# A two-block layer kernel: the one-hot rows that enter the weight-building products are first copied to one contiguous run per token

## The chip, the core and the metric

One core of one Trainium2 chip. The time is device microseconds of one execution; the median of three runs of the kernel before is 2320.74 us. Beside it stands one profiled execution. Engines are named as the profile names them: PE (TensorE matmul), PEld (TensorE weight load, overlapping PE), DVE (VectorE), ACT (ScalarE), POOL (GpSimd), SP (SyncE, which issues most loads).

## The reference

Two transformer blocks, one after the other, on one sequence of 512 tokens of width 1024. The change lies in the last part of the second block, a product-key mixture of single-neuron experts (PEER):

```
q = (xb @ w_query).reshape(TOKEN_BLOCK, P_HEADS, 2, P_HALF)
s = einsum('thpk,hpnk->thpn', q, sub_keys)
sv, si = top_k(s, P_TOPK)
... eidx: the 16 best of the 256 pairs of each of 8 heads; g: softmax of their scores
u = u_tab[eidx]
act = gelu(einsum('td,thkd->thk', xb, u))
return einsum('thk,thkd->td', g * act, v_tab[eidx])
```

There are 16384 experts; an expert number is a pair of two numbers below 128, and each token picks 8 x 16 of them.

## The kernel before, in words

All matrix products run on PE with operands split into a high and a low part (32-bit, three products for one), except the ones of this change, which take 16-bit operands.

The experts are done in two ways. For the first 128 tokens, rows of `u_tab` and `v_tab` are gathered (line 1484) and multiplied on DVE (lines 1492 and 1510). For the other 384 tokens (three tiles b = 1, 2, 3 of 128), all 16384 experts are computed densely. `dense_S` (line 1570) makes one S tile: it loads 128 rows of `u_tab`, ACT casts the high part `uh` (1575), POOL makes the low part `ul` (1576), PE runs 24 products of 384 columns (lines 331, 332, 334) and ACT applies gelu (1580). Of the 128 S tiles, 59 are made ahead of the second product (`more_S`), and wait on chip or in DRAM (`Sd`). The second product (line 1826) multiplies each S tile by the weight that each token gives each expert and by `v_tab`.

That weight of every expert per token, a matrix of 128 x 128 for each of 384 tokens, is what the changed code builds. For 16 tokens at a time, four at a time within them:

- `make(b, n)` (line 1601): DVE writes `oh` (line 1612), for both halves of the expert number the one-hot row over 128 candidates, 4 tokens side by side in the innermost dimension, and `ow` (line 1615), the first half's one-hot row times the score in two 16-bit parts. Four instructions of each per call; four buffers each (`OB`).
- `build(b, n)` (line 1618): for each four tokens, PE runs 8 products (line 1626) of 128 x 128 into one bank `gps`: the stationary operand is a token's second one-hot row, the moving one a part of `ow`. Both are read with a step of 4 elements (8 bytes), since 4 tokens lie side by side. ACT evacuates the bank into `gst` (line 1628), and ACT's queue stores 16 tokens to DRAM (`Gd`, line 1629).

24 builds make 96 banks and 768 products. The loop at line 1702 makes the rows for the next build, then builds the present one, then asks for 3, 2 or 1.5 S tiles (b = 1, 2, 3), and for b = 1 and 2 also runs one head of the next tile's top-16 search on DVE (`topk_head`). At the end of each tile's search, `route_end` transposes the numbers on PE (1647, 1648), and ACT and DVE make `tT` (1649 to 1651), from which the next `make` reads. In b = 3 at n = 4 the gathered rows still waiting are used up on DVE (line 1492).

The order in which each engine runs its instructions is fixed before the run by the tile framework's planner, from its own estimates of cost; it need not be that of the code (in the trace `oh`, `oh`, `ow`, `ow` alternate in pairs, where the code has `oh`, `ow`). `pin` keeps some in the code's order. Each engine runs its queue in order and waits on semaphores.

```
for k in range(2):                                            # 1624
    for t in range(4):
        PE.matmul(ps[:, t * 128:(t + 1) * 128], o[:, 1, :, t], w[:, k, :, t], start=k + t == 0,
                  stop=k + t == 4, skip_group_check=True)     # 1626
S.mul(st[:, :, t4 * 4:t4 * 4 + 4], ps.rearrange("p (t i) -> p i t", i=128), 1.0 / GS)   # 1628
```

Of the kernel before, what the change touches and what calls it, by code (L numbers as in the profile page):

```python
# [11 lines left out]
F16 = mybir.dt.float16  # L12
# [8 lines left out]
D = 1024  # L21
KC = 8
SEQ = 512
META = 16
T = 512
# [3 lines left out]
LA = 6  # L29
# [8 lines left out]
GLAG = 3  # L38
# [61 lines left out]
def layout(a):  # L100
    """the inputs in the order in which the kernel reads them: feature-major activations, weights in blocks of 128
    or 256 columns, one column per 128 entries of a vector"""
# [44 lines left out]
def tile_blocks(  # L147
# [26 lines left out]
    # ---------------------------------------------------------------- constants  # L174
# [72 lines left out]
    def small_constants():  # L247
        nc.scalar.dma_start(out=cf, in_=a["cf"])
        with tc.tile_pool(name="init", bufs=1) as ip:
# [4 lines left out]
            # sqrt(w^2 + eps) of the first block's last norm  # L254
# [28 lines left out]
    # ---------------------------------------------------------------- matrix products  # L283
# [12 lines left out]
    def weights(w, m, n, eng=None, step=None):  # L296
        """a block [128, m, n] of weights and its split, step of the m at a time"""
# [14 lines left out]
    def ahead(w, hi, lo, eng=None, step=None):  # L312
        """a block of 128 columns split ahead of its turn, in other room than that of the weights"""
# [13 lines left out]
    def chain(ps, ab, first=True, last=True):  # L327
        """sum of a^T b over the pairs of split operands (a, b); a's low parts are needed last"""
# [7 lines left out]
    def gemm_fm(ws, X, N, evac, kouter=None, after=None, mid=None, eng=lambda s: None):  # L336
        """feature-major: evac(s, psum[128, N]) per block s of 128 columns; the first two blocks step by step together
        where kouter, the kind of their banks (their operand X is just coming in); after(s, raw weights);
        mid(k) after step k of these; eng(s): which engine makes the low parts of the weights"""
# [23 lines left out]
    def meta_fm(raw, um):  # L363
        """feature-major projection of the 16 meta tokens: psum[128, 16]"""
        ps = tr_tile("meta")
        for k in range(KC):
            PE.matmul(ps[:, 0:META], raw[:, k, :], um[:, k, :], start=(k == 0), stop=(k == KC - 1))
        return ps[:, 0:META]

    def gemm_tm(w, X, evac, after=None, n=256):  # L370
        """token-major: evac(b, psum[128 tokens, n]) for the n columns of w [128, KC, n]; one b per step"""
# [16 lines left out]
    def newton(ps, eps, n):  # L388
        """ps [128, n]: sums of D squares; -2 D / sqrt(ps / D + eps), its logarithm's estimate refined once"""
# [10 lines left out]
    def newton_small(ss, eps, n, tmp):  # L400
        """ss [128, m] SBUF: sums of n squares -> 1 / sqrt(ss / n + eps) in ss"""
# [8 lines left out]
    class SquareSum:  # L410
        """sums over the features of (x * wcol)^2: all chunks but the last are added up on the way"""
# [34 lines left out]
    def scaled_X(xr, wcol):  # L446
        """split of xr * wcol"""
# [5 lines left out]
    class Early:  # L453
        """two blocks of weights times X that still lacks the factor and the shift of its norm: flush(s) adds what the
        shift brings and evacuates"""
        def __init__(self, ws, X, cols, shift, evac, room, factor):
            """shift [128, KC]; room(s): two tiles of half a block's size; factor() makes the norm's factor"""
# [26 lines left out]
    def norm_X(X, xr, rs, wcol, bcol, keep=None):  # L484
        """split of xr * rs * wcol + bcol (wcol carries the factor of rs)"""
# [15 lines left out]
    def modulation(ip):  # L501
        """one step per call of next: rows of ada_w"""
# [25 lines left out]
        for n in range(6 * D // AW):  # L528
# [11 lines left out]
            # the sum over the partitions: 32 at a time by a transpose, the four of them by a product  # L540
# [17 lines left out]
    # ---------------------------------------------------------------- block 1  # L558
# [13 lines left out]
    def sigmoid(dst, src):  # L572
        """exp(-ln(1 + exp(-src))), src at least -43"""
# [4 lines left out]
    def gla(X, um, Y, sp, rs, rsT, hooks):  # L578
        """returns the parts in the order in which they may run; rs, rsT: factors of the columns and rows of products
        with X"""  # L580
# [35 lines left out]
        def decay():  # L616
            # decay: running sums of log sigmoid, restarted every 128 tokens
# [15 lines left out]
        def proj_v(h):  # L633
            """the values; with the first half of their columns, the 16 of the decay's first product"""
# [27 lines left out]
        def state():  # L662
            # state after the meta tokens
# [1202 lines left out]
```

## Time and profile before

| | us |
|---|---|
| three runs | 2320.26, 2320.74, 2330.18 |
| their median | 2320.74 |
| span of the profiled execution, first to last instruction | 2316.9 |
| median less span | 3.8 |
| busy on PE, DVE, POOL, ACT in the profiled execution | 2196.2, 1781.6, 1031.0, 903.7 |
| busy of line 1626 in it (768 products) | 98.0 |

The profile gives no other time of its own execution than the span. It is read by stretches: the builds lie between 1106 and 1420 us of the span; before it stand the other layers, behind it the second product up to the end. A matmul's end in the trace is modelled, so the pace of PE is read from starts.

### The profile page before, as it was taken

How to read it: one execution, taken by the hardware profiler on the slowest of the kernel's cores; microseconds unless marked ns; L12 is line 12 of the kernel's file. 1: busy time of each engine (PE TensorE's matmuls, PEld its weight loads, DVE VectorE, ACT ScalarE, POOL GpSimd, SP SyncE). 2: the span in 40 equal slices, each digit the busy share in tenths (PEclk: the TensorE clock that was granted, in tenths of full speed). 3: DMA queues.
4: the chain of work that ended last, by engine and by line, in shares of the span. 5: the costliest groups of instructions: out<-in, count | busy, mean ns of one | idle time of the engine just before them, and what ended most of it. 6: DMA issues, size and time to landing. Idle time of an engine off the chain costs nothing.

```text
span 2316.9 us, 30890 instructions
## 1 busy us (share of the span) xinstructions
PE 2196.2 (95%) x11067; PEld 1865.7 (81%) x11067; DVE 1781.6 (77%) x3276; ACT 903.7 (39%) x1529; POOL 1031.0 (44%) x609
## 2 busy tenths in 40 slices
PE   9999999999989999997979999999999999999996
PEld 7777777877768777776969998776789999999994
DVE  5876657654485787899999965565679998989987
ACT  3345542233334664533334443333333333333333
POOL 1310221121150003512334434777788787778776
PEclk9999999999999999998989999999999999999998
DMA  5111357553222212631545667888889999999983
GB/s 178 59 39 46 118 161 244 179 168 106 81 92 78 64 61 85 227 98 62 186 135 189 212 222 238 285 264 281 273 316 327 338 336 322 340 339 330 340 305 136
DMA packets 181268, 455.09 MB, mean 196 GB/s; under 512 B 16597, under 2 KB 82006, under 8 KB 178042
## 3 DMA queue, kind: packets, MB, share of 16 engines
q1 hardware_dynamic: 82080, 252.58, 32.7%
q0 software_dynamic: 36864, 134.23, 16.2%
q10 hardware_dynamic: 62170, 66.30, 8.3%
q8 instruction: 87, 1.43, 0.3%
q14 instruction: 67, 0.55, 0.1%
HBM read 412.63 MB, written 39.79 MB: 195 GB/s over the span
## 4 chain that ended last, share of the span: by engine, by line
PE 42%; DVE 25%; issue 16%; POOL 9%; DMA 5%; ACT 2%; ACTq 0%; POOLq 0%; DVEq 0%; SPq 0%
PE do L1826 6%; POOL gt L1484 5%; PE mm L331 4%; PE mm L332 3%; PE mm L334 3%; POOL vl L1807 3%; PE S L331 3%; PE S L332 3%; PE S L334 3%; DVE oh L1612 3%; PE ff L331 2%; PE ff L334 2%; PE ff L332 2%; DVE ow L1615 2%; DVE vacc L1510 1%
## 5 line engine op out<-in xcount | busy, mean ns | idle before, releaser
L331 PE MATMUL S<-xhi,uh 128*128 128x384 f32 x1024 | 355.8, 347 | 5.9 <-ACT sg L1580 4.7
L332 PE MATMUL S<-xlo,uh 128*128 128x384 f32 x1024 | 352.4, 344 | 0.0
L1576 POOL TENSOR_TENSOR ul<-ur,uh 128x1024 fp32r<-128x1024 f32 x59 | 157.7, 2677 | 289.8 <-ACT uh L1575 208.6
L289 DVE TENSOR_TENSOR wlo<-raw,whi 128x1024 fp32r<-128x1024 f32 (+4 forms) x150 | 175.6, 1175 | 129.9 <-ACT whi L288 100.4
L1826 PE MATMUL do<-vh,wl 128*128 128x512 f32 x768 | 245.7, 399 | 15.2 <-DVE wl L1814 15.1
L1826 PE MATMUL do<-vl,wh 128*128 128x512 f32 x768 | 245.9, 400 | 10.9 <-POOL vl L1807 10.7
L1826 PE MATMUL do<-vh,wh 128*128 128x512 f32 x768 | 245.9, 400 | 1.1 <-ACT vh L1806 0.9
L1510 DVE SCALAR_TENSOR_TENSOR vacc<-gt,act,vacc 128x1024 f32<-128x1024 f32 x127 | 211.0, 1661 | 41.9 <-DMA gt<-in_v_dram,eidx 40.2
L288 ACT CAST whi<-raw 128x1024 fp32r<-128x1024 f32 (+4 forms) x152 | 146.1, 969 | 231.9 <-PE ff L332 107.2
L1492 DVE SCALAR_TENSOR_TENSOR gt<-gt,h2t 128x1024 f32<-128x1024 f32 x118 | 176.4, 1503 | 65.3 <-DMA gt<-in_u_dram,eidx 65.1
L331 PE MATMUL mm<-xhi,whi 128*128 128x512 f32 x544 | 219.8, 404 | 0.7 <-DVE xc L1127 0.7
L1575 ACT CAST uh<-ur 128x1024 fp32r<-128x1024 f32 x128 | 134.4, 1050 | 215.5 <-DMA ur<-in_ut_dram 115.0
L332 PE MATMUL mm<-xlo,whi 128*128 128x512 f32 x544 | 217.2, 399 | 0.0
L1807 POOL TENSOR_TENSOR vl<-vr,vh 128x1024 fp32r<-128x1024 f32 x64 | 174.8, 2732 | 80.7 <-ACT vh L1806 72.7
L331 PEld LDWEIGHTS S<-xhi,uh 128*128 128x128 f32 x1024 | 199.0, 194 | 9.5 <-ACT sg L1580 5.0
L332 PEld LDWEIGHTS S<-xlo,uh 128*128 128x128 f32 x1024 | 198.8, 194 | 3.2
L334 PE MATMUL S<-xhi,ul 128*128 128x384 f32 x1024 | 201.1, 339 | 0.0
L1807 POOL TENSOR_TENSOR vl<-vx,vh 128x1024 fp32r<-128x1024 f32 x64 | 169.3, 2645 | 61.5 <-ACT vh L1806 60.7
L1813 ACT CAST wh<-sg 128x384 fp32r<-128x384 f32 x128 | 65.5, 513 | 316.9 <-PE do L1826 210.1
L1826 PEld LDWEIGHTS do<-vh,wl 128*128 128x128 f32 x768 | 145.1, 190 | 53.6 <-DVE wl L1814 20.7
L1826 PEld LDWEIGHTS do<-vl,wh 128*128 128x128 f32 x768 | 145.7, 191 | 50.8 <-POOL vl L1807 17.0
L1484 POOL DMA_INDIRECT gt<-in_v_dram,eidx x128 | 166.7, 1303 | 32.5 <-issue 25.4
(481 smaller groups left out, 4819.8 us busy)
## 6 DMA issues: line engine op xcount, KB each, us to landing
ur<-in_ut_dram SPq DMA_DIRECT2D x128, 512.0 KB, 5.5
raw<-in_w_ff_dram SPq DMA_DIRECT2D x64, 512.0 KB, 3.6
vr<-in_v_dram SPq DMA_DIRECT2D x64, 512.0 KB, 4.6
vx<-in_v_dram SPq DMA_DIRECT2D x64, 512.0 KB, 7.6
aw<-in_ada_w_dram SPq DMA_DIRECT2D x64, 384.0 KB, 3.8
Gd<-gst ACTq DMA_DIRECT2D x24, 1024.0 KB, 4.3
gti<-Gd ACTq DMA_DIRECT2D x90, 256.0 KB, 5.0
raw<-in_w_in_dram SPq DMA_DIRECT2D x32, 512.0 KB, 4.4
```

The costliest lines, as they stand in the source:

```text
L288: S.copy(hi, src)
L289: (eng or V).tensor_tensor(out=lo, in0=src, in1=hi.bitcast(F32), op=OP.subtract)
L331: PE.matmul(ps, ah, bh, start=first and i == 0, stop=False, skip_group_check=True)
L332: PE.matmul(ps, ah, bl, start=False, stop=False, skip_group_check=True)
L334: PE.matmul(ps, al, bh, start=False, stop=last and i == n - 1, skip_group_check=True)
L1484: pin(G.indirect_dma_start(out=gt, out_offset=None, in_=tab, in_offset=bass.IndirectOffsetOnAxis(ap=eidx[:, s:s + 1], axis=0)))
L1492: ins = V.scalar_tensor_tensor(gt, gt, 1.0, h2t, op0=OP.mult, op1=OP.mult, accum_out=act[:, s:s + 1])
L1510: V.scalar_tensor_tensor(vacc, gt, act[:, s:s + 1], vacc, op0=OP.mult, op1=OP.add)
L1575: S.copy(uh, ur)
L1576: eng.tensor_tensor(out=ul, in0=ur, in1=uh.bitcast(F32), op=OP.subtract)
L1807: G.tensor_tensor(out=vl, in0=vr, in1=vh.bitcast(F32), op=OP.subtract)
L1826: PE.matmul(po[2 * tb + h], w[:, ts], v[:, h * 512:(h + 1) * 512], start=first and n == 0, stop=last and n == 127, skip_group_check=True)
```

## The change

In `make`, a tile `oc` [128, 4, 128] of 16-bit entries with four buffers is added, and an ACT copy that reads the second one-hot rows (step of 4 elements) and writes each token's 128 entries in one run. `build` takes the stationary operand from `oc`. The loops over the two parts and the four tokens are exchanged: a token's two products, with the same stationary operand, follow each other. The moving operand is read as before. The first and last product of a bank are the same ones. The diff also blanks comments, which changes no instruction; lines behind 1616 move down by three.

```diff
                 w = gp.tile([128, 2, 128, 4], F16, name="ow", bufs=OB)
                 V.tensor_tensor(out=w, in0=o[:, 0:1].to_broadcast([128, 2, 128, 4]), in1=cols(2, 2), op=OP.mult)
-                made.append((o, w))
+
+                oc = gp.tile([128, 4, 128], F16, name="oc", bufs=OB)
+                S.copy(oc, o[:, 1].rearrange("p i t -> p t i"))
+                made.append((oc, w))
...
-                for k in range(2):
-                    for t in range(4):
-                        PE.matmul(ps[:, t * 128:(t + 1) * 128], o[:, 1, :, t], w[:, k, :, t], start=k + t == 0,
+                for t in range(4):
+                    for k in range(2):
+                        PE.matmul(ps[:, t * 128:(t + 1) * 128], o[:, t, :], w[:, k, :, t], start=k + t == 0,
                                   stop=k + t == 4, skip_group_check=True)
```

## Rows read from the trace of the kernel before

**Rows 1.** The page, part 1: busy time, share of the span, instructions.

```profile
PE 2196.2 (95%) x11067; PEld 1865.7 (81%) x11067; DVE 1781.6 (77%) x3276; ACT 903.7 (39%) x1529; POOL 1031.0 (44%) x609
```

**Rows 2.** Windows by stretch: stretch, its us, busy per engine, TensorE clock, DMA.

```profile
1099.00:1203.00 104.00, 99.66 (x615) 95.01 (x616) 103.96 (x288) 37.97 (x60) 40.75 (x15) 0.94 0.51 178
1203.00:1216.50 13.50, 0.33 (x3) 0.04 (x1) 13.50 (x71) 3.02 (x4) 2.35 (x1) 0.54 0.06 12
1217.00:1304.80 87.80, 87.80 (x565) 86.47 (x564) 87.73 (x310) 39.24 (x59) 42.01 (x14) 0.98 0.56 198
...
1324.00:1378.00 54.00, 53.46 (x349) 52.41 (x350) 32.23 (x44) 22.25 (x34) 16.79 (x7) 0.97 0.70 242
1378.00:1405.00 27.00, 22.29 (x155) 21.41 (x153) 25.87 (x26) 11.14 (x19) 15.37 (x6) 0.94 0.68 234
1405.00:1432.00 27.00, 27.00 (x160) 26.78 (x158) 13.40 (x21) 10.08 (x16) 9.61 (x4) 0.93 0.57 199
1432.00:2317.00 885.00, 844.13 (x4000) 730.50 (x3998) 713.86 (x726) 305.57 (x425) 673.58 (x377) 0.98 0.86 301
```

**Rows 3.** Waits, 1100 to 1432: who waited for whom, us, times, longest.

```profile
POOL ul L1576 <- ACT uh L1575: 175.2, 33, 15.3
...
PE tr L1647 <- DVE ef L1407: 13.2, 1, 13.2
PE gps L1626 <- DVE ow L1615: 12.7, 10, 2.5
```

**Rows 4.** Waits, 1324 to 1432, the same columns.

```profile
DVE oh L1612 <- PE gps L1626: 22.0, 7, 7.3
...
PE gps L1626 <- DVE ow L1615: 6.4, 3, 2.5
```

**Rows 5.** Chain that ended last, 1324 to 1432: start, us, what.

```profile
by line: PE gps L1626 23.2%; PE S L331 18.4%; PE S L332 18.1%; PE S L334 16.7%; DVE oh L1612 9.7%; DVE gv L1492 7.3%; DVE ow L1615 4.5%; DVE gt L1492 2.1%; issue 0.1%
...
1336.49 3.81 PE gps L1626 x32
...
1348.64 3.80 PE gps L1626 x32
...
1387.11 7.84 DVE gv L1492 x6
```

**Rows 6.** Line 1626: ns min/median/max, first and last start, forms.

```profile
L1626 PEld LDWEIGHTS <-oh x768: 112/117/152, 1105.8 to 1418.9; 128*128 128x128 f16 x192
```

**Rows 7.** Line 1663, the same columns: a load of 32-bit columns.

```profile
L1663 PEld LDWEIGHTS ks<-skT,q x128: 186/192/339, 946.7 to 1057.3; 128*128 128x128 f32 x128
```

**Rows 8.** Timeline from 1399.0, PEld: the first two loads of a build.

```profile
1398.99 0.15 PEld L1626 LDWEIGHTS <-oh 128*128 128x128 f16 x2 [2.51 <-DVE ow L1615]
```

**Rows 9.** Timeline of PE from 1217.2, after an idle stretch: start, us, what.

```profile
1217.22 1.48 PE L1626 MATMUL gps<-ow,oh 128*128 128x128 f16 x11
...
1219.24 0.52 PE L331 MATMUL S<-xhi,uh 128*128 128x384 f32 x1
```

**Rows 10.** Windows around it: stretch, us, busy, clock (after POOL).

```profile
1217.20:1218.50 1.30, 1.30 (x14) 1.28 (x11) 1.30 (x10) 1.02 (x4) 0.00 (x0) 0.50 0.31 122
...
1336.30:1340.00 3.70, 3.70 (x33) 3.62 (x32) 2.52 (x2) 2.29 (x4) 2.39 (x1) 1.00 0.50 169
```

**Rows 11.** Timeline of PE from 1344.3: two products of an S tile.

```profile
1344.31 0.34 PE L331 MATMUL S<-xhi,uh 128*128 128x384 f32 x1
1344.48 0.34 PE L332 MATMUL S<-xlo,uh 128*128 128x384 f32 x1
```

**Rows 12.** Costliest groups of ACT: count | busy, mean ns | idle, releasers.

```profile
L1628 ACT ACTIVATE gst<-gps 128x512 f32<-128x512 f32 x96 | 55.1, 600 | 36.2 <-PE gps L1626 32.0 <-DMA Gd<-gst 3.1 <-ACT sx L1580 0.9
...
L288 ACT CAST yhi<-Y 128x512 fp32r<-128x512 f32 x16 | 9.0, 619 | 3.1 <-DVE Y L819 2.8 <-PE tr L1249 0.3
```

**Rows 13.** Line 1612, columns as for line 1626: the one-hot rows on DVE.

```profile
L1612 DVE TENSOR_TENSOR oh<-io,tT x96: 666/683/2902, 1101.1 to 1410.2; 128x1024 f16<-128x1024 f16 x96
```

**Rows 14.** Timeline of ACT from 1344.5: a cast for a later S tile.

```profile
1344.90 1.04 ACT L1575 CAST uh<-ur 128x1024 fp32r<-128x1024 f32 x1
```

## The prediction, made before the result was known

> **What bounds the kernel now.** I read the page first: PE is busy for 2196.2 us of 2316.9, DVE for 1781.6, ACT for 903.7 [rows 1]. That is an average; what the change is worth is read from the stretches in which the builds run. The windows by stretch [rows 2] show three kinds of time. From 1099 to 1304.8 us DVE is busy in every microsecond (103.96 of 104.00, 13.50 of 13.50, 87.73 of 87.80): it makes the one-hot rows and runs the top-16 search of the next tile. PE works beside it, nearly full, and then stands still for 13 us from 1203 to 1216.5. The waits [rows 3] say why: its longest wait is 13.2 us, in the transposes of `route_end`, for the search on DVE. All its other waits there (12.7 us, 10 times) are for `ow`, again DVE. DVE's waits for PE, 22.0 us in 7 times, all lie behind 1324 [rows 4]. So up to about 1324 DVE sets the pace, and a faster PE would only wait longer.
>
> From 1324 on it is the other way round, as the search is over: PE is busy 53.46 of 54.00 us while DVE idles, then a stretch of 27 us in which DVE uses up gathered rows, then 27.00 of 27.00 on PE, and 844 of 885 us in the second product [rows 2]. The chain of waits from 1324 to 1432 has line 1626 as its largest part, 23.2% of 108 us, which is 25 us [rows 5]. One build there takes 3.81 us for 32 products, 119 ns each; so 25 us are about 208 of the 768 products. The other 560 lie where DVE sets the end. That number, **208 products**, is what any change of PE's pace in the builds is multiplied by.
>
> **Part 1: the stationary operand becomes contiguous.** What sets the 119 ns? A record of a 16-bit load lasts 112 to 117 ns [rows 6], almost the pace, so the load looks guilty. Three rows speak against it. First, a load of the same 128 columns in 32 bits, contiguous, lasts 186 ns at the least [rows 7]: the strided 16-bit load is already 74 ns shorter. Second, where a build begins after a wait, two loads are issued at once and both are over 0.15 us after the first began [rows 8]; one alone takes 0.112, so the second needs the load path for not more than 38 ns. A path that can take a load every 38 ns doesn't set a pace of 119. Third, the pace doesn't follow PE's clock: after the idle stretch, at a granted clock of 0.50 (the lower level, 1.2 GHz), 11 products take from 1217.22 to the next line's start in the same 0.11 to 0.12 us each as at 1.00 (2.4 GHz) [rows 5, 9, 10], while the S tile's products behind them last 0.52 us instead of 0.34 [rows 9, 11]. What is left is something fixed in time: the reading of the moving operand, which has the same step of 8 bytes and keeps it, the issue of a load and a product by turns, or a product that waits for the whole latency of its load. Only the last could gain from contiguous weights.
>
> The bounds: at best the pace becomes that of the columns themselves. Two products of 384 columns start 0.17 us apart [rows 11], 0.45 ns a column, so 128 columns are 58 ns. Then 208 x (119 - 58) = 12.7 us go from the path; 34 us more go from PE in stretches where it would only wait. At worst nothing goes, or a product that reads the same bank columns twice running gets slower; the S tile accumulates 24 products into the same columns at the pace above, so that I exclude. I take 0, since the three rows all say that the load isn't what is waited for, and keep 12.7 for the range.
>
> Here a rule speaks against the change as well. The Trainium skill, page "TensorE: Matmul & The Clock Gate", section "Weight-path perf modes", says that the fast weight load is chosen for 128 weights that aren't 32-bit, whether they are packed or strided, up to steps of about a thousand elements. By it the load before is already the fast one and the copy changes nothing: the sum stays as it is; by the rows alone up to 12.7 us are open. The 74 ns agree with the rule.
>
> **Part 2: a token's two parts in turn.** The same weights now come twice running. Lines 331 and 332 do that already (one `uh`, two moving operands) and yet PE's products and PEld's loads are equal in number, 11067 each [rows 1]: no product goes without its load. I expect 768 loads as before. If the second load were left out, it would at most free 38 ns for half of 208 products, 4 us. I take 0.
>
> **Part 3: 96 copies on ACT.** [128 x 512] costs 600 ns out of PSUM and 619 ns as a cast within SBUF [rows 12]; the copy's step on the reading side is in neither row. I take 0.6 us: 96 x 0.6 = 58 us more on ACT. Between the two kinds of cost: hidden altogether (0), or all in the path (58). ACT is busy 38 of 104, 39 of 88 and 22 of 54 us in the stretches [rows 2], and gets 2.4 us per build of 10 to 17; so there is room, and what counts is who waits for it. PE now waits for `ow` and for `oc`. DVE writes two `oh` and then two `ow` (0.68 us for an `oh` [rows 13], an `ow` is of the same size), so the second `oh` is done 1.4 us before the second `ow`, and its copy at 0.6 us fits in between. It counts only where PE was already waiting for `ow`, 10 times [rows 3], and of these only for the three behind 1324 [rows 4]. I take 1 us; the bounds are 0 and 10 x 0.6 = 6 us. The copies also stand in ACT's queue in front of other work: the casts `uh`, behind which POOL waits 175.2 us in all [rows 3], the gelu that frees the S banks and the evacuation of `gps`. PE has not one wait for `uh`, `ul` or a bank from 1100 to 1432, so that cover is thick: POOL stands idle for the casts, and nobody for POOL. I take 0; what it costs if the cover is gone is the second rival. No DMA is added; the store of `gst` keeps its place behind the fourth evacuation, and SP's queue is not touched.
>
> **Part 4: the buffers.** An `oh` buffer was free when PE had read it; now when `ow` and `oc` have been made. The 22.0 us in which DVE's `oh` waits for PE [rows 4] therefore end earlier, but the next `ow` waits for the same products, so DVE runs only two `oh` further ahead. DVE has slack there. 0.
>
> **Sum.** 0 + 0 + 1 + 0 + 0 = +1 us on a span of 2316.9; the median of the runs is 3.8 us over the span and I keep that: 2320.7 + 1, about **2321.5 us**. The planner's new order may move an S tile (24 products, 4.2 us) across the 13 us of idle time in either direction, so this case's own range is 2316 to 2327.
>
> **Rival 1, the load was in the way after all** (a product waits for its load's whole latency, and a contiguous one is much shorter). For it: a load's record, 117 ns, almost equals the pace. Against it: the three rows above. It gives 12.7 us at the most: 2320.7 + 1 - 12.7 = 2309; half of it, 2315. The Trainium skill, same page, section "Back-to-back issue gap", gives about 81 ns per pair of load and product at 128 columns; an estimate by that is 208 x 38 ns = 8 us less, 2314. No row here shows that pace.
>
> **Rival 2, slower: ACT's queue stands behind a copy that waits for DVE.** ACT is in order; a copy placed early stands at its head until DVE has written `oh`, and behind it wait `uh` and the gelu that frees one of two S banks; then PE waits. For it: before 1304 DVE is never free, so what waits for it waits long, and the planner's estimates set the order without knowing the real delays. Against it: PE idles 13 us there anyhow, and behind 1324 DVE is ahead. It decides where ACT is held for longer than the head start of the casts: the one at 1344.90 [rows 14] serves the S tile behind the build at 1348.64 [rows 5], which starts 7.5 us later. If each of the 8 last builds passes its four copies on, 8 x 2.4 = 19 us: 2320.7 + 19 = 2340; if that happens in two, 2325.
>
> **Rival 3, the change doesn't do what it says:** the second load of a token isn't issued and the loads halve. That gives at most 4 us less, 2317.5, hardly to be told from no change.
>
> **How the numbers follow.** A difference of 0.5%, 11.6 us, is about what can be told from no change here. Chances: forecast 0.55, rival 1 0.23, rival 2 0.15, rival 3 0.07. Rival 1 crosses 0.5% only near its end, so about half of it is faster, 0.12, and I give 0.05 to an order that happens to suit PE better: faster 0.17. Slower: most of rival 2, 0.14. Within 0.5%: the rest, 0.69. The range takes in rival 1 to its end (2308.5) and rival 2 to about two thirds of its price (2333).
>
> **What would show it.** Right: line 1626 with 768 loads, starts still 0.11 to 0.12 us apart, 3.8 us per build in the chain; 96 ACT copies of about 0.6 us; the stretch from 1203 to 1216 still waiting for DVE's search. Rival 1: a build of 32 products in 2 to 3 us and shorter loads. Rival 2: a row in which PE waits for ACT's `oc`, `uh` or gelu. Rival 3: fewer than 768 loads. The forecast is wrong if the builds behind 1324 get shorter by over a third, or if a stretch before 1324, where DVE is full, changes its length.

## The result and the profile after

The changed kernel is slower: median 2339.03 us of four runs (2337.93 to 2346.66) against 2321.07 of the kernel before (2320.26 to 2330.18, measured again beside it). The ratio is 1.0076, 95% interval 1.0054 to 1.0098. That is 18 us, outside the predicted range (2308.5 to 2333.0).

The page, part 1, of the changed kernel, beside [rows 1]:

```profile
PE 2198.4 (94%) x11067; PEld 1867.6 (80%) x11067; DVE 1780.1 (76%) x3276; ACT 954.1 (41%) x1625; POOL 1032.8 (44%) x609
```

PE, DVE and POOL do the same work; ACT has 96 instructions and 50 us more. The windows by stretch, the same stretches and columns as [rows 2]:

```profile
1099.00:1203.00 104.00, 88.82 (x547) 85.62 (x547) 104.00 (x351) 50.09 (x83) 32.79 (x12) 0.91 0.42 147
1203.00:1216.50 13.50, 11.39 (x64) 11.34 (x65) 13.50 (x50) 10.07 (x19) 5.33 (x2) 0.75 0.42 160
1217.00:1304.80 87.80, 71.03 (x444) 69.25 (x443) 87.73 (x278) 41.59 (x68) 36.27 (x12) 0.88 0.46 160
...
1324.00:1378.00 54.00, 51.16 (x353) 50.03 (x352) 31.47 (x42) 32.81 (x57) 15.88 (x6) 0.96 0.52 179
```

From 1217 to 1304.8 PE is busy for 71.03 us where it was busy for all of 87.80, at a granted clock of 0.88 where it was 0.98. Who waited for whom, 1100 to 1432, beside [rows 3]:

```profile
ACT oc L1618 <- DVE oh L1612: 37.4, 15, 8.4
...
PE gps L1629 <- DVE ow L1615: 15.3, 3, 9.6
...
PE S L331 <- ACT uh L1575: 12.3, 4, 5.6
PE tr L1650 <- DVE ef L1407: 11.8, 1, 11.8
PE S L331 <- ACT sx L1580: 5.8, 1, 5.8
PE gps L1629 <- ACT gst L1631: 5.2, 3, 2.4
```

Before, PE waited for nothing but DVE. Now it waits for ACT 23.3 us (12.3 + 5.8 + 5.2), and for `ow` three times up to 9.6 us instead of ten times up to 2.5. (The 11.8 us are the first tile's search; before, that wait ended at 1099.03, just outside the window. The 13.2 us of the second tile are gone: PE comes late to it.) The first row is new and no small thing: ACT stood 37.4 us with a copy at the head of its queue for which DVE had not yet made `oh`.

Not all of PE's waits for ACT come from the copies, though. What stood at the head of ACT's queue before three of them, in the timelines of ACT and PE (start, length, what, idle time before it and its releaser):

```profile
1137.26 0.64 ACT L1618 COPY oc<-oh 128x512 f16<-128x512 f16 x1 [3.44 <-DVE oh L1612]
1138.91 0.69 PE L331 MATMUL S<-xhi,uh 128*128 128x384 f32 x1 [3.67 <-ACT uh L1575]
...
1201.85 0.31 ACT L1639 ACTIVATE gsm<-gsm 128x128 f32<-128x128 f32 x1 [12.39 <-DVE gsm L1638]
...
1405.83 1.04 ACT L1575 CAST uh<-ur 128x1024 fp32r<-128x1024 f32 x1 [8.55 <-DMA ur<-in_ut_dram]
```

Behind a copy that stands for `oh`, PE waits 9.1 us: 3.67 and 2.63 for `uh` at 1139 and 1161, 2.40 for `gst` at 1131, 0.41 for `uh` at 1226. The 5.8 us for `sx` (the gelu) come behind `gsm`, an ACT instruction of the search that waits 12.39 us for DVE. The 5.6 us for `uh` come behind a load of `ur`, for which the cast waits 8.55 us. No copy is in front of these two. Before the other 2.8 us, for `gst`, copies stand that wait 0.3 us at most.

The two groups of the change, the copies and the loads, the latter beside [rows 6]:

```profile
L1618 ACT COPY oc<-oh x96: 631/654/693, 1104.9 to 1425.0; 128x512 f16<-128x512 f16 x96
...
L1629 PEld LDWEIGHTS <-oc x768: 95/115/127, 1106.6 to 1436.6; 128*128 128x128 f16 x192
```

Still 768 loads; a contiguous one can take 95 ns where a strided one took 112, and yet the products of a build start 115 ns apart on average instead of 118. From first to last load the builds take 330.0 us (1106.6 to 1436.6) instead of 313.1 (1105.8 to 1418.9 [rows 6]), and what is behind them 900.1 instead of 898.0. So the loss lies in the builds; the span is 2336.7 against 2316.9.

One place of the worst stretch, in the timelines of PE, DVE and ACT:

```profile
1279.72 3.87 PE L1629 MATMUL gps<-ow,oc 128*128 128x128 f16 x32 [9.57 <-DVE ow L1615]
1283.34 0.67 PE L331 MATMUL S<-xhi,uh 128*128 128x384 f32 x1
1283.80 0.52 PE L332 MATMUL S<-xlo,uh 128*128 128x384 f32 x1
```

```profile
1276.75 4.63 DVE L1615 TENSOR_TENSOR ow<-oh,tT 128x1024 f16<-128x1024 f16 x4
1281.30 1.88 DVE L1612 TENSOR_TENSOR oh<-io,tT 128x1024 f16<-128x1024 f16 x3
```

```profile
1282.07 0.66 ACT L1618 COPY oc<-oh 128x512 f16<-128x512 f16 x1 [7.40 <-DVE oh L1612]
```

DVE now makes four `ow` and then four `oh` of the next make in one block, where it alternated in pairs before: the planner chose another order for the changed program. The block came late for this build, and PE stood still for 9.57 us; the build ran at a granted clock of 0.50, and the S tile behind it began at this lower level too (0.52 us a product, as in [rows 9]). ACT meanwhile stood for 7.40 us at a copy. Of the 16.77 us that PE lacks from 1217 to 1304.8, 14.74 are waits for `ow` (5.17 and 9.57).

DVE itself loses nothing. Its last step of the search (`ef`) and PE's transposes behind it, first in the kernel before, then in the changed one (first and last start):

```profile
L1407 DVE TENSOR_REDUCE ef<-oh x32: 659/670/687, 958.9 to 1314.4; 128x32 f32<-128x512 bf16 x32
L1647 PE MATMUL tr<-ci,ef x6: 272/419/477, 1099.0 to 1320.5; 128*128 128x128 f32 x6
...
L1407 DVE TENSOR_REDUCE ef<-oh x32: 655/670/689, 960.4 to 1311.5; 128x32 f32<-128x512 bf16 x32
L1650 PE MATMUL tr<-ci,ef x6: 270/271/474, 1101.2 to 1337.1; 128*128 128x128 f32 x6
```

The last search ends 2.9 us earlier than before, and PE comes to its transposes 16.6 us later: PE is late with its own work.

### The profile page after: what moved, and what is told of

Read it like the earlier page. It is cut to its first block, busy times and chain, and to the rows that moved or that the text cites. A ratio compares the mean times of both kernels' runs of the same rounds, so it can differ in the third digit from the quotient of the medians.

```text
span 2336.7 us, 31148 instructions
## 1 busy us (share of the span) xinstructions
PE 2198.4 (94%) x11067; PEld 1867.6 (80%) x11067; DVE 1780.1 (76%) x3276; ACT 954.1 (41%) x1625; POOL 1032.8 (44%) x609
## 4 chain that ended last, share of the span: by engine, by line
PE 44%; DVE 21%; issue 15%; POOL 9%; DMA 8%; ACT 2%; SPq 0%; ACTq 0%; POOLq 0%; DVEq 0%
PE do L1829 6%; POOL gt L1484 4%; PE mm L331 4%; PE mm L334 4%; PE mm L332 4%; PE S L331 3%; PE S L332 3%; PE S L334 3%; DMA gt<-in_v_dram,eidx 2%; PE ff L331 2%; PE ff L334 2%; PE ff L332 2%; POOL vl L1810 2%; PE gps L1629 2%; DMA sg<-Sd 2%
## 5 line engine op out<-in xcount | busy, mean ns | idle before, releaser
L1829 PE MATMUL do<-vh,wl 128*128 128x512 f32 x768 | 245.9, 400 | 17.5 <-DVE wl L1817 17.5
L1510 DVE SCALAR_TENSOR_TENSOR vacc<-gt,act,vacc 128x1024 f32<-128x1024 f32 x127 | 216.6, 1706 | 39.3 <-DMA gt<-in_v_dram,eidx 37.6
L1816 ACT CAST wh<-sg 128x384 fp32r<-128x384 f32 x128 | 65.4, 513 | 309.7 <-PE do L1829 196.3
```

The source lines that it names most:

```text
L1510: V.scalar_tensor_tensor(vacc, gt, act[:, s:s + 1], vacc, op0=OP.mult, op1=OP.add)
L1829: PE.matmul(po[2 * tb + h], w[:, ts], v[:, h * 512:(h + 1) * 512], start=first and n == 0, stop=last and n == 127, skip_group_check=True)
```

## The experiments

Two explanations stood against each other: the order theory (the planner's new order costs) and the queue theory (the copies hold up ACT). To separate them, a program's own order was carried into another one: at the end of the kernel every instruction of an engine is tied behind the one that is to precede it (issue order only, no wait). `ranks` is the order read from the other program; the copies are left to the planner unless it says otherwise.

```diff
+    def in_order(engine, ranks):
...
+        for p, q in zip(n, n[1:]):
+            tc.add_manual_dep(mine[q], mine[p].name, mybir.DependencyInfo(mybir.DependencyClass.NoSync, mybir.DependencyReason.DATA), reason="order")
```

All results at a glance. A ratio goes against runs of the kernel before made beside that run (medians 2320.09 to 2322.95), so it is not the quotient of two medians of this table. Builds: from the first to the last load of the build products; behind: from there to the end of the span. Both are of one profiled execution, which need not lie at the median: x9's took 2327.62 us and x10's 2352.85, 7 us over theirs, x16's 2341.22, 8 us under it.

| run | median us | ratio to before, 95% | builds | behind |
|---|---|---|---|---|
| before | 2321.07 | | 313.1 | 898.0 |
| after | 2339.03 | 1.0076 (1.0054 to 1.0098) | 330.0 | 900.1 |
| x1 after, order of before | 2347.20 | 1.0100 (1.0081 to 1.0119) | 327.6 | 915.0 |
| x2 before, order of after | 2361.84 | 1.0166 (1.0146 to 1.0187) | 354.7 | 904.1 |
| x10 as x2, 7 `oh` | 2346.31 | 1.0113 (1.0087 to 1.0139) | 337.6 | 907.3 |
| x16 after, `oh` freed by PE | 2349.34 | 1.0123 (1.0093 to 1.0152) | 323.9 | 910.2 |
| x5 copies behind `uh` | 2337.00 | 1.0068 (1.0049 to 1.0088) | 321.8 | 905.0 |
| x8 copies at their place | 2327.92 | 1.0029 (1.0012 to 1.0046) | 308.4 | 913.1 |
| x17 as x1, copies without wait | 2322.96 | 0.9999 (0.9983 to 1.0015) | 309.7 | 903.1 |
| x3 loops exchanged | 2322.13 | 0.9998 (0.9982 to 1.0015) | 312.6 | 903.8 |
| x4 after, flat moving operand | 2331.80 | 1.0031 (1.0017 to 1.0045) | 318.4 | 904.6 |
| x6 roles exchanged, as x5 | 2328.10 | 1.0028 (1.0014 to 1.0043) | 316.6 | 904.5 |
| x9 roles exchanged, as x8 | 2320.43 | 0.9999 (0.9981 to 1.0017) | 304.7 | 915.3 |
| x7 no copy | 2350.08 | 1.0122 (1.0099 to 1.0144) | 340.8 | 901.3 |
| x14 copies on POOL | 2364.63 | 1.0183 (1.0159 to 1.0208) | 352.7 | 903.9 |
| x11 before, 4 KB more | 2323.05 | 1.0009 (0.9990 to 1.0029) | 312.9 | 900.1 |
| x12 as x8, 3 buffers | 2340.52 | 1.0081 (1.0058 to 1.0103) | 333.3 | 898.9 |
| x13 as x9, 3 buffers | 2339.24 | 1.0076 (1.0054 to 1.0098) | 325.8 | 905.2 |
| x15 as x9, `ur` first | 2324.46 | 1.0013 (0.9995 to 1.0031) | 302.0 | 911.1 |

x3 has the order of the kernel before and still 903.8 us behind the builds: one profiled execution cannot tell differences of 6 us there from none.

### Order or queue

**x1_after_order_before.** The changed kernel with the edit

```diff
+    in_order(mybir.EngineType.DVE,
...
+    in_order(mybir.EngineType.PE,
...
+    in_order(mybir.EngineType.Activation,
...
```

> The changed kernel with the copies and the contiguous stationary operand kept, but the instructions of DVE, PE and ACT (all of ACT's but the 96 copies, which the planner puts in between) held in the order in which they stand in the kernel before. Order theory (the loss lies in the order that the planner chose for the changed program, which gives PE its ow late): 2318 to 2325 us, and PE waits for ow for under 1 us at a time from 1216 to 1320. Queue theory (the copies' 0.65 us each, or a copy at the head of ACT's queue that waits for DVE, holds up PE in any order): 2330 to 2340 us, with waits of PE for uh, sx or oc.

It is slower still, 2347.20, above the ranges of both theories. The order theory alone falls: PE's waits for `ow` are gone (0.9 us), but its waits for ACT stay. Waits of x1, 1100 to 1432, and below them a piece of its chain (start, us, what):

```profile
ACT oc L1619 <- DVE oh L1613: 84.2, 38, 7.7
...
PE S L331 <- ACT uh L1575: 18.4, 7, 5.5
...
PE gps L1630 <- DVE ow L1616: 0.9, 1, 0.9
```

```profile
1343.68 1.87 PE gps L1630 x16
...
1345.58 0.69 DVE ow L1616
1346.27 0.61 DVE oh L1613
...
1346.96 0.66 ACT oc L1619
...
1348.12 1.05 ACT uh L1575
...
1349.21 0.69 PE S L331
```

This is the mechanism in one piece. Half a build must be done before DVE may write the next `ow`; behind that `ow` in DVE's queue stands an `oh`; for that `oh` a copy waits at the head of ACT's queue; behind the copy stands the cast `uh`; and PE, done with its build, waits for `uh`.

**x2_before_order_after.** The kernel before, with the same lines for all five engines and the order of the changed kernel.

> The kernel before, without any copy and with the strided stationary operand, but the instructions of all five engines held in the order in which they stand in the changed kernel. Order theory: 2334 to 2345 us, with PE waiting for ow for 5 to 10 us at a time between 1217 and 1290 as in the changed kernel. Queue theory: 2318 to 2326 us, since no copy is there.

2361.84, above the order theory's range: without any copy, the planner's new order costs 40 us. In it DVE waits 44.3 us for PE to release `oh`, and PE 43.9 us for `ow`. **x10** gives it more `oh`:

```diff
-                o = gp.tile([128, 2, 128, 4], F16, name="oh", bufs=OB)
+                o = gp.tile([128, 2, 128, 4], F16, name="oh", bufs=7)
```

> x2_before_order_after (no copies, the order of the changed kernel on all engines) with seven buffers of oh instead of four, so that DVE needn't wait for PE to release one (45.1 us in x2). If the changed kernel's time is its order, eased by the early release of oh: 2332 to 2342 us, as the changed kernel. If the order by itself costs more than that: 2345 us or more; if the order is harmless once oh is released early: 2318 to 2326 us.

2346.31, on the second branch. Its waits, 1100 to 1432:

```profile
PE gps L1627 <- DVE ow L1616: 32.5, 8, 9.0
DVE oh L1613 <- PE gps L1627: 31.8, 10, 11.1
...
PE S L331 <- ACT sx L1580: 7.0, 1, 7.0
...
PE S L331 <- ACT uh L1575: 5.6, 1, 5.6
```

Without copies the order costs 26 us with seven buffers of `oh` and 40 with four. So that order is bad in itself. But seven do not do what they were to do: DVE still waits 31.8 us for PE to release `oh`, once for 11.1 us. What the order costs where `oh` comes free as early as in the changed kernel was therefore not measured. The rows show one thing more: the long waits for `sx` (behind `gsm`) and `uh` (behind its load) that the changed kernel has stand here too, in a program without a copy; in x2 they are 7.7 and 7.6 us.

**x16** takes the early release away from the changed kernel (and leaves the order to the planner):

```diff
-                        PE.matmul(ps[:, t * 128:(t + 1) * 128], o[:, t, :], w[:, k, :, t], start=k + t == 0,
+                        PE.matmul(ps[:, t * 128:(t + 1) * 128], (o[:, 1, :, t] if t + k == 4 else oc[:, t, :]), w[:, k, :, t], start=k + t == 0,
```

> The changed kernel with one of a bank's eight products (the first token's... the last one to finish the bank) still reading the strided rows of oh, so that a buffer of oh is freed by PE as in the kernel before; copies, loops and everything else as in the changed kernel, the order left to the planner. If the early release of oh is why the planner's order costs (it lets it run four oh a whole make ahead of their ow): 2320 to 2327 us. If the copies' stage on ACT is why: 2335 us or more, with PE waiting for ow, oc, uh or sx for over 20 us between 1100 and 1430.

2349.34, within the range of the stage on ACT. But the planner gave this program a third order: DVE makes `oh` and `ow` in pairs again, as in the kernel before, and nowhere in blocks of four. So x16 does not hold the changed kernel's order against it. It shows two other things: the blocks go away when only the early release does, with all copies kept; and under pairs the copies cost as much as in x1. Its waits, 1100 to 1432:

```profile
ACT oc L1618 <- DVE oh L1612: 86.8, 41, 8.5
...
PE S L331 <- ACT uh L1575: 15.5, 8, 3.6
```

PE's waits for `ow` (5.6 us), `uh` and `sx` (1.4) make 22.5 us, as that theory had it.

### The copy's place and the copy's time

**x5_copies_behind_uh.** As x1; the copies of builds 8 to 23 are tied into ACT's order.

```diff
+        for c in copies[4 * m:4 * m + 4]:
+            tc.add_manual_dep(mine[c], last, no, reason="order")
```

> As x1_after_order_before, but in ACT's queue the four copies of each build from the ninth on stand behind the casts uh of the S tiles ahead of that build, where the planner had put them in front of a cast. The same 96 copies, the same 0.65 us each, the same order on DVE and PE. Head-of-line theory (a copy that waits for DVE's oh, whose buffer or whose queue place waits for PE, keeps uh from PE): 2320 to 2328 us, with no wait of PE for uh of over 1 us behind 1324 (x1 had five of 1.8 to 2.5 us). If the copies' own time on ACT is what costs: 2343 to 2350 us as in x1.

2337.00, between the two: a miss for both. From 1216 on PE now waits not for `uh` but for `oc` (15.7 us), 0.34 us at most builds, 2.06 where one S tile lies between, once 4.95: `uh` itself cannot start before PE has left the S tile before it, and the copies behind it come too late.

**x8_copies_at_their_place.** The same edit with other places: in the third tile right behind the evacuation of the build before.

> As x5_copies_behind_uh, but in the third tile (builds 16 to 23) a build's four copies stand in ACT's queue right behind the evacuation of the build before it, ahead of the gelu and the cast of the S tile in between, and the copies of builds 14 and 15 stand ahead of what waits for the end of DVE's search. In x5 PE waited 0.34 us for oc at most builds, 2.06 at those with one S tile in front, 4.95 and 1.47 at builds 14 and 15: 17 us in all from 1219 on. Placing theory (neither the copies' 0.65 us nor the pace costs anything, only where a copy stands among uh, sx and gst in ACT's queue): PE's waits for oc and uh fall under 4 us in all, 2321 to 2327 us. If ACT's occupancy counts by itself: other work of ACT comes late instead, and it stays at 2333 us or more.

Half a hit: the time is 1 us above the range, and PE's waits for `oc` and `uh` are 9.5 us in all, not under 4. In the builds nothing is lost any more: 308.4 us, 4.7 less than before, with the same 96 copies. Its waits, 1100 to 1432:

```profile
PE S L331 <- ACT uh L1575: 7.3, 2, 4.7
...
PE gps L1630 <- DVE ow L1616: 4.3, 4, 2.6
...
PE gps L1630 <- ACT oc L1619: 2.2, 7, 0.4
```

Yet the median is 2327.92: what the builds gave comes back behind them (913.1 us), see below.

**x17_copies_without_wait.** The queues of x1, instruction by instruction, with copies of a constant:

```diff
-                S.copy(oc, o[:, 1].rearrange("p i t -> p t i"))
-                made.append((oc, w))
+                S.copy(oc, io4.rearrange("p i t -> p t i"))
+                made.append((o, w))
...
-                        PE.matmul(ps[:, t * 128:(t + 1) * 128], o[:, t, :], w[:, k, :, t], start=k + t == 0,
+                        PE.matmul(ps[:, t * 128:(t + 1) * 128], o[:, 1, :, t], w[:, k, :, t], start=k + t == 0,
```

> The queues of DVE, PE and ACT instruction by instruction as in x1_after_order_before, the 96 copies at the same places among them and of the same size, but each copy reads a constant (io4, with the same step of four) in place of oh, and the products read the strided rows of oh again: no copy waits for DVE, and no product waits for a copy. If the loss of x1 is the wait at the head of ACT's queue: 2319 to 2326 us, with no wait of PE for uh or sx of over 1 us. If it is the 58 us that the copies occupy ACT: 2340 to 2350 us as x1.

2322.96, no difference from the kernel before, and 24 us below x1. Its copies take as long as those of x1 (655 ns), at the same places in ACT's queue:

```profile
L1619 ACT COPY oc<-io x96: 639/658/704, 1104.3 to 1397.6; 128x512 f16<-128x512 f16 x96
...
  ACT gst L1632: 0.8, 2
  ACT sx L1580: 0.8, 2
```

Under the group stands what its engine waited for before it: next to nothing, where x1 waited 84.2 us for `oh` and 17.5 us for PE to free an `oc`. So 96 copies, 50 us more of ACT's busy time, cost nothing that can be measured; what costs is that a copy holds the queue while it waits. x17 differs from x1 in three more things, all as in the kernel before: its products read strided rows, they do not wait for a copy, and PE frees `oh`. But strided rows are the slower ones by 3 ns, x1 has no wait of PE for `oc`, and x8 frees `oh` early as x1 does and loses nothing in the builds. (The trace of x17 puts one wait of 2.55 us before a build down to `uh`; at that build the kernel before waits 2.19 us for `ow`.)

### What sets the pace of the products

**x3_swap_loops.** The kernel before, loops exchanged:

```diff
-                for k in range(2):
-                    for t in range(4):
+                for t in range(4):
+                    for k in range(2):
```

> The kernel before with the two loops exchanged and nothing else; the order of every engine is otherwise that of the kernel before. Both theories: 2321 us, 768 loads, 117 to 119 ns a product. If a token's two parts in turn cost or save anything by themselves, it shows here as a pace that differs by over 5 ns.

No difference, 768 loads, 118 ns. **x4_after_flat_moving:**

```diff
-                        PE.matmul(ps[:, t * 128:(t + 1) * 128], o[:, t, :], w[:, k, :, t], start=k + t == 0,
+                        PE.matmul(ps[:, t * 128:(t + 1) * 128], o[:, t, :], w[:, k].rearrange("p i t -> p (i t)")[:, t * 128:(t + 1) * 128], start=k + t == 0,
```

> The changed kernel with the moving operand read as 128 elements side by side instead of with a step of four: the products then take wrong entries of ow, so the weights of the experts are not those of the reference. Order of all engines as in the changed kernel. If the step of the moving operand sets the pace (stride theory): 60 to 85 ns a product, a build of 32 products in under 2.8 us instead of 3.65, and the time a few us shorter, about 2333. If something fixed per load and product sets it: 113 to 115 ns as now, and 2339 us.

PE's timeline of x4: the next line's product starts at 1345.63, so 32 products take 1.76 us, 55 ns each.

```profile
1343.87 1.96 PE L1629 MATMUL gps<-ow,oc 128*128 128x128 f16 x32
1345.63 0.42 PE L331 MATMUL S<-xhi,uh 128*128 128x384 f32 x1
```

The step of the moving operand sets the pace; the stride theory is shown. Whether the stationary operand then matters too is told by a version that computes the right sums with the roles exchanged, **x6_roles_exchanged** (copies as in x5):

```diff
-                V.tensor_tensor(out=w, in0=o[:, 0:1].to_broadcast([128, 2, 128, 4]), in1=cols(2, 2), op=OP.mult)
+                V.tensor_tensor(out=w, in0=o[:, 1:2].to_broadcast([128, 2, 128, 4]), in1=cols(2, 2), op=OP.mult)
...
-                S.copy(oc, o[:, 1].rearrange("p i t -> p t i"))
+                S.copy(oc, o[:, 0].rearrange("p i t -> p t i"))
...
-                        PE.matmul(ps[:, t * 128:(t + 1) * 128], o[:, t, :], w[:, k, :, t], start=k + t == 0,
+                        PE.matmul(ps[:, t * 128:(t + 1) * 128], w[:, k, :, t], o[:, t, :], start=k + t == 0,
```

> x5_copies_behind_uh with the roles of the two halves exchanged: the copied, contiguous one-hot rows become the moving operand, and the stationary operand is ow, made from the second half's one-hot rows and read with the step of four. The same sums, so the result is unchanged. If only the step of the moving operand sets the pace: 56 to 60 ns a product although the stationary operand is strided again, a build in 1.8 us, and 208 x 60 ns = 12 us less than x5, about 2310 us, if the S tiles' operands come in time; 2320 if they don't. If a strided stationary operand is felt once the moving one is fast: 80 to 115 ns a product, 2316 to 2324 us.

The time is 2328.10, 9 us below x5, not 12; PE waits for copies within its builds (26.4 us for `oc` from 1100 to 1432, 15.7 in x5). **x9_roles_exchanged_placed** has the same edit on x8:

> x8_copies_at_their_place with the roles of the two halves exchanged as in x6: contiguous one-hot rows as the moving operand, strided ow as the stationary one. If x8 comes out at 2321 to 2327: 208 x 59 ns = 12 us less, 2309 to 2316 us, faster than both kernels. If S tiles then wait for uh (ACT and DMA behind a faster PE): about 2318 us.

PE's timeline and the loads of x9:

```profile
1350.15 1.98 PE L1630 MATMUL gps<-oc,ow 128*128 128x128 f16 x32
1351.93 0.42 PE L331 MATMUL S<-xhi,uh 128*128 128x384 f32 x1
```

```profile
L1630 PEld LDWEIGHTS <-ow x768: 110/113/152, 1105.8 to 1410.5; 128*128 128x128 f16 x192
```

1.78 us for 32 products, 56 ns, with strided loads of 113 ns: the stationary operand's step does not matter. The builds take 304.7 us, but the median, 2320.43, is that of the kernel before, above the 2309 to 2316 of the first branch: PE now waits 15.3 us for `uh` and 20.1 for `ow` (1100 to 1432).

**x7_no_copy** lets DVE write the contiguous rows itself:

```diff
+                of = gp.tile([128, 4, 128], F16, name="of", bufs=OB)
+                V.tensor_tensor(out=of, in0=iof.rearrange("p (o i) -> p o i", o=1).to_broadcast([128, 4, 128]),
+                                in1=tT[:, 0, ts].rearrange("p (t o) -> p t o", o=1).to_broadcast([128, 4, 128]), op=OP.is_equal)
```

> The roles exchanged as in x6, but without any copy: DVE itself writes the first half's one-hot rows contiguous per token (an extra is_equal of 128 x 512, while the strided oh shrinks to 128 x 512), and the planner chooses the order. If the new instruction, whose second operand is one number repeated along the row, runs at the pace of oh (0.35 us for 512): DVE as before, ACT as before, 56 to 60 ns a product, 2305 to 2314 us. If it runs at half that pace (0.6 us): 96 x 0.25 = 24 us more on DVE, two thirds of it where DVE sets the pace, 2318 to 2330 us.

2350.08, worse than either end. The new instruction takes 0.68 us and the shorter `oh` 0.41 (both at the end of this document), so DVE is busy for 39 us more than in the kernel before, not 24; the planner's order is another one too. **x14_roles_copies_on_POOL** (three buffers of `oh` and `oc`, the planner's order):

```diff
-                S.copy(oc, o[:, 0].rearrange("p i t -> p t i"))
+                G.tensor_copy(oc, o[:, 0].rearrange("p i t -> p t i"))
```

> The roles exchanged, three buffers of oh and oc, the copies on POOL instead of ACT, and no order given: the planner chooses, and its order on DVE and PE comes out close to that of the kernel before. If it is the order and ACT's queue that cost: 2308 to 2318 us. If POOL in its turn holds the low parts ul behind a copy that waits for DVE, or slows DVE's instructions beside it: 2322 to 2335 us.

2364.63, the highest median here. The queue of POOL stands at the copies, and PE waits for them. A copy takes 1.07 us there (median), and DVE is busy for 45 us more with as many instructions; which of these costs how much was not separated. Waits, 1100 to 1440:

```profile
POOL oc L1618 <- DVE oh L1612: 83.2, 26, 8.1
...
PE gps L1629 <- POOL oc L1618: 43.7, 16, 5.6
```

### Behind the builds

x8 and x9 shorten the builds by 4.7 and 8.4 us and lose 15 to 17 behind them in the profiled executions; by the medians (8 us more than the kernel before, and none) it is about 12 and 9, an estimate. One suspect was the room that `oc` takes: with 4 KB more, the planner lets all six loads of the built weights (line 1791 of the changed kernel) stand behind the last build (in the changed kernel they start between 1444.3 and 1446.9). **x11_before_4KB_more:**

```diff
+        pad = gp.tile([128, 1024], F32, name="pad")
+        G.memset(pad[:, 0:1], 0.0)
```

> The kernel before with one unused tile of 4 KB per partition (as much as the four oc buffers) in the pool of the builds, and nothing else. In the kernel before that pool begins 1088 bytes above the pool of the second product; 4 KB more make the two overlap, and the six first loads of the built weights (line 1787) move behind the last build, as in the changed kernel. Room theory (part of the loss is the room that oc takes, by way of these late loads): the builds end as before at about 1419 us of the span, and the first products behind them wait: 2324 to 2330 us. If the late loads are hidden: 2318 to 2323 us.

Not to be told from no difference. **x12_placed_3_buffers** and **x13_roles_placed_3_buffers** take 3 KB from x8 and x9:

```diff
-                o = gp.tile([128, 2, 128, 4], F16, name="oh", bufs=OB)
+                o = gp.tile([128, 2, 128, 4], F16, name="oh", bufs=3)
...
-                oc = gp.tile([128, 4, 128], F16, name="oc", bufs=OB)
+                oc = gp.tile([128, 4, 128], F16, name="oc", bufs=3)
```

> x8_copies_at_their_place with three buffers of oh and of oc instead of four (3 KB less, so that the two pools no longer overlap and five of the six first loads of the built weights go out during the builds again). Room theory: the builds take no longer than in x8, the loss of 7 to 8 us behind them is gone, 2317 to 2322 us, no slower than the kernel before. If the loss behind the builds has another cause: 2326 to 2330 us as x8.

> x12_placed_3_buffers with the roles of the two halves exchanged, so that the moving operand is contiguous (56 ns a product). Room theory: 7 to 8 us less than x9_roles_exchanged_placed, 2308 to 2315 us, faster than both kernels. If the S tiles' loads or casts bound the builds by now: 2316 to 2320 us.

Both missed. In x12 the loss behind the builds is indeed gone (898.9 us), but DVE then waits 33.6 us (1215 to 1440) for copies to free `oh`, and the builds take 25 us more. **x15_roles_ur_before_gti** leaves the buffers and moves two loads on SP:

```diff
+    for g in gls:
+        tc.add_manual_dep(g, uls[60].name, no, reason="order")
```

> x9_roles_exchanged_placed with one thing more: on SP's queue the loads ur of the first two S tiles of the second product go ahead of the six loads of the built weights (gti), which wait for the builds' room and held these ur up (in x9 ACT waited 2.7 us for gti and PE 1.3 to 2.6 us at a time for wh, vh and vl right behind the builds, and the first 150 products of the second product took 43.5 us instead of 35.6). If this queue is what x9 gave its gain back to: 5 to 8 us less than x9, 2311 to 2316 us. If it is something else: 2318 to 2322 us.

Missed too: the builds are the shortest of all (302.0 us), and now the second product's first factor comes late. Waits of x15, 1405 to 1440:

```profile
DVE sg L1817 <- DMA gti<-Gd: 13.1, 1, 13.1
...
PE do L1833 <- ACT wh L1820: 7.2, 1, 7.2
```

So in x15 a faster build phase runs into the loads of the built weights, and no version measured here is faster than the kernel before. Whether the room is part of the loss in x8 and x9 is not shown: in x12 it is gone together with the short builds, x13 has 905.2 us with the same room, and alone, in the kernel before, the room costs nothing that shows (x11). What would free both was not tried.

## Why the prediction was wrong

**What held.** Part 1: the load was not in the way; the pace went from 118 to 115 ns, which on 208 products is 0.6 us, and the moving operand's step was rightly named among what is left (x4, x9). Part 2: 0, with 768 loads (x3). Part 3's size of a copy: 0.65 us against 0.6. Rivals 1 and 3 did not happen. (Rival 1's end is 2309 by its own sum; the 2308.5 of the range has no other source.)

The Trainium skill's rule on the fast weight load ("TensorE: Matmul & The Clock Gate", section "Weight-path perf modes"), packed or strided alike, agrees with x4 and x9: 55 and 56 ns. Its 81 ns for 128 columns (section "Back-to-back issue gap") is seen in no run at a granted clock of 1.00: with the moving operand strided it is 113 or more, with it contiguous 56 or less.

**One step that failed: "PE has not one wait for `uh`, `ul` or a bank from 1100 to 1432, so that cover is thick", and the 0 put on it in Part 3.** The row was right and the conclusion wrong. No wait means only that the casts came in time in a queue without copies. The prediction's own rival 2 had a head start of 7.5 us for one cast behind 1344; in the changed kernel the cast right behind the copy at 1137.26 has none, and PE waits 3.67 us for it. Measured: PE waits 23.3 us for ACT in the changed kernel, 0 before; 9.1 of these stand behind a copy that waits for `oh`. Under the old order the waiting at the head of the queue is worth 24 us (x1 against x17, in which the same copies do not wait).

**The other, which has the longer waits in the changed kernel: the planner's order, which "may move an S tile (24 products, 4.2 us)" in either direction.** Without copies that order costs 26 us (x10) to 40 us (x2), six to ten times as much. In the changed kernel its waits are the 15.3 us for `ow` and the 11.4 us for `sx` and `uh` that x2 and x10 have too. Keeping the old order is no way out either: with the copies where the planner then puts them it costs 25 us (x1). Both together are the loss in the builds: with the old order and the copies at other places it is gone (x8). How the 18 us divide between them stays open. The old waits, 25.9 us, are gone in exchange, and no run has the changed kernel's order with copies that do not wait.

Why the planner chose blocks of four is shown in part: in x16 they go when `oh` is no longer freed early. Part 4 named that early release and put it at 0 by asking what DVE would do in the old order, not what order the planner would then choose.

**Under both lies "up to about 1324 DVE sets the pace, and a faster PE would only wait longer".** DVE is full up to 1304.8 before and after, but PE had next to nothing to spare there: it stood for 17.5 us from 1099 to 1304.8 [rows 2], and in the changed kernel for 34.1. PE must make up later for what it misses, as its transposes at 1337.1 instead of 1320.5 show.

**Rival 2** had one of the two mechanisms, with a chance of 0.15. That its 2340 comes near the time is luck: it adds up builds behind 1324, while in the changed kernel PE's missing work lies between 1217 and 1304.8 (16.77 us not busy, 0 before), and there it is waits for `ow`. "PE idles 13 us there anyhow" was counted against it; the new waits used those 13.2 us up and went on. Behind 1324, too, the held queue does what it said, but in x1, where the old order is kept.

**The signs that the prediction named** for its being wrong came: "a row in which PE waits for ACT's `oc`, `uh` or gelu", and, as the later transposes show for PE, "a stretch before 1324, where DVE is full, changes its length".

## What to carry to other kernels

An instruction put on an idle engine costs what stands behind it while it waits, not its own time: compare the longest time that its producer can be late with the head start of the work queued behind it, before calling the engine's idle share a cover. Then look at what stood at the head of the queue before each new wait: half of the waits for ACT here had no copy in front and stand in the same order without copies as well. An engine that works beside a full one need not have time to spare: count the time for which it stands. Where a planner sets the order, a new stage is a new order of everything; test the change under the old order and the old program under the new one, to know which of the two is paid for. And before an operand is made contiguous, find out which of the two the products wait for.

## What was not expected of the hardware

- A moving operand with a step of 8 bytes (16-bit entries) costs half of the pace: 32 products of 128 columns take 3.62 us in the changed kernel (1337.36 to 1340.98), 113 ns each, and 1.76 us in x4, 55 ns each, both at a granted clock of 1.00. The stationary operand's step costs 3 ns at the slow pace and 1 at the fast one.
- The strided pace does not follow the clock and the contiguous one does: at a granted clock of 0.50 the changed kernel's build at 1279.72 takes the same 3.62 us, and x4's at 1280.82 takes 3.33 us, 104 ns a product instead of 55.
- Loads of 113 ns do not hinder products every 56 ns (x9): the length of a load's record is no bound on the pace.
- On DVE a comparison whose second operand is one number repeated along the row takes as long for 512 elements (679 ns) as one of 1024 with the ordinary operand; the ordinary one of 512 takes 414. The two groups of x7:

```profile
L1612 DVE TENSOR_TENSOR oh<-io,tT x96: 400/414/2625, 1100.4 to 1437.3; 128x512 f16<-128x512 f16 x96
...
L1616 DVE TENSOR_TENSOR of<-iof,tT x96: 662/679/2821, 1100.9 to 1437.6; 128x512 f16<-128x512 f16 x96
```
